# A hybrid mixer trunk on one core: the low parts of the w_up weights made by ScalarE and an accumulating DMA instead of VectorE

## The chip, the cores and the metric

One core of a Trainium2 chip runs the whole program; the other cores are idle. The metric is the device time in microseconds (us) of one execution. The engines are TensorE (PE, with its weight loads listed apart as PEld), VectorE (DVE), ScalarE (ACT), GpSimd (POOL) and SyncE (SP), which here only issues DMAs. Lower is better.

## The reference

One layer of a trunk over 512 tokens of width 1024, all in float32. Four mixers (a pooling branch, a dilated attention, a stick-breaking attention, a state-space branch) are gated and summed; then comes the feed-forward part that the change touches:

```
gu = hn @ w_up[l]                                   # 512x1024 @ 1024x5632
h = silu(gu[..., :FFN_HIDDEN]) * gu[..., FFN_HIDDEN:]
x = x + h @ w_down[l]                               # 512x2816 @ 2816x1024
return rmsnorm(x, final_norm_g)
```

## The kernel before

Every large product is done in three TensorE passes. A float32 operand is split in a high part, its value rounded to the shorter type float32r, and a low part, the float32 value minus the high part. `mm3` (L195) multiplies high by high, high by low activation, and low weight by high activation, and adds the three in one PSUM bank. For each block of 128 rows of the weight (a k tile) these are three matmuls in this order, so that the low weights are first read by the third matmul.

Weights come as a stream of chunks, listed in `specs`: those of w_in, of the gates and branches, of w_out, and then twice 11 chunks of w_up (2048 columns per partition, 1 MB) followed by 8 of w_down (1408 columns). A w_up chunk holds 8 k tiles of 256 columns; its first 128 columns make the gate product `m_fg`, the others the product `m_fu` (`s_fu` in the first two chunks). That is 24 matmuls each, 48 for a chunk; a w_down chunk is 33 matmuls into `m_d`.

`next_chunk` (L186) sets the order of the stream. When chunk c is about to be multiplied, it issues the load of a chunk two ahead into one of two `raw` buffers (`load_next`, on the queue of SP), and the split of chunk c + 1 (`split_next`) into one of two buffers `hi` and one of two `lo`. The split is done in two halves, k tiles 0 to 3 and 4 to 7: ScalarE writes `hi` with a cast, VectorE writes `lo` with a subtraction that reads `raw` and `hi`. As there are two buffers of each, the split of chunk c + 1 can't begin before TensorE is done with chunk c - 1. A `raw` buffer is loaded again when the last reader of it, so far the subtraction, is done. The order on each engine is that in which the program is written (a manual schedule).

Around a w_up chunk j the other work is `glu_up` (L1144): VectorE scales `m_fg` to `tg`, ScalarE applies Silu, VectorE scales `m_fu` to `tu` and multiplies, and the result is split in `hh` (ScalarE) and `hl` (VectorE). GpSimd does nothing but some memsets ahead of all this.

Of the kernel before, what the change touches and what calls it, by code (L numbers as in the profile page):

```python
# [13 lines left out]
AF = mybir.ActivationFunctionType  # L14
ALU = mybir.AluOpType
AX = mybir.AxisListType
PSUM = bass.MemoryType.PSUM
# [26 lines left out]
CST_CNT = 512  # L44
CST_W = CST_CNT + 64

N_SLOTS = 61  # [128, 512] tiles in the rotating pool
N_RAW = 2  # weight chunks loaded ahead
N_PM = 3  # PSUM banks of the main stream; the rest serve side work
S5_RATE = 0.9  # steps of the S5 branch per tick  # L50
SB_RATE = 1.0  # steps of the stick-breaking branch per tick
MAX_LAG = 4.0  # backlog of DVE and ACT (us) at which side work pauses
H_WAIT = 4  # ticks between the S5 rotation tables and their use
SB_T = 2  # steps from stick-breaking scores to their transposes
SB_O = 2  # steps from the transposes to the outputs
DIL_O = 1  # the same for the dilated branch
N_WARM = 8  # products on constants that bring up the PE clock while the first loads run
N_HALVED = 2  # last tiles of w_down done by token halves
BC_AT = 7  # k tiles of the last product before the first half is broadcast
W0_PIECES = {0: 1, 1: 3, 4: 2, 6: 2}  # first k tile: number of k tiles, pieces of the first weight chunk  # L60
S5_PAR = 48
S5_W = S5_PAR + 4 * 256

# [20 lines left out]
def _advance(clock, key, cost):  # L84
    clock[key] = cost + (clock[key] if key == "pe" else max(clock[key], clock["pe"]))
# [3 lines left out]
def hybrid_trunk(ctx: ExitStack, tc: tile.TileContext, a: dict, out: bass.AP):  # L89
    nc = tc.nc  # L90
    G, SY = nc.gpsimd, nc.sync
    clock = {"pe": 0.0, "v": 0.0, "a": 0.0}
    V = _Paced(nc.vector, lambda n: _advance(clock, "v", 0.09 + 1.04e-3 * n))
    A = _Paced(nc.scalar, lambda n: _advance(clock, "a", 0.20 + 0.83e-3 * n))
    PE = _Paced(nc.tensor, lambda n: _advance(clock, "pe", max(0.42e-3 * n, 0.1)))
    ctx.enter_context(tc.manual_schedule())

    gp = ctx.enter_context(tc.tile_pool(name="consts", bufs=1))
    sp = ctx.enter_context(tc.tile_pool(name="slots", bufs=N_SLOTS))
    wp = ctx.enter_context(tc.tile_pool(name="weights", bufs=2))  # L100
    sm = ctx.enter_context(tc.tile_pool(name="small", bufs=1))
    pm = ctx.enter_context(tc.tile_pool(name="pmain", bufs=N_PM, space=PSUM))
    pa = ctx.enter_context(tc.tile_pool(name="pside", bufs=8 - N_PM, space=PSUM))
    dp = ctx.enter_context(tc.tile_pool(name="scratch", bufs=1, space=DRAM))
    mixers = ExitStack()
# [5 lines left out]
    def nm_(nm):  # L111
        uid[0] += 1
        return f"{nm}_{uid[0]}"
# [11 lines left out]
    def side_ps(nm):  # L125
        return pa.tile([P, T], F32, tag="at", name=nm_("s_" + nm))
# [9 lines left out]
        V.tensor_tensor(r_(lo), src, hi, ALU.subtract)  # L136
        return r_(hi), r_(lo)

    # ------------------------------------------------------- weight stream
    specs = (  # L140
        [("w_in", 17 + c, 2048) for c in range(2)]
        + [("w_in", 2 + 3 * w + g, 2048) for g in range(3) for w in range(3)]
# [21 lines left out]
    loaded, ready = [], []  # L164
    used = [0]

    def load_next(pieces=1):
        key, i, n = specs[len(loaded)]
        raw = wp.tile([P, 2048], F32, tag="raw", name=nm_("raw"), bufs=N_RAW)
        for s in range(pieces):  # L170
            sl = slice(s * n // pieces, (s + 1) * n // pieces)
            SY.dma_start(raw[:, sl], a[key][i][:, sl])
        loaded.append((raw, n))

    def split_next(pieces=2):
        raw, n = loaded[len(ready)]
        ch = Chunk()
        ch.hi = wp.tile([P, 2048], F32R, tag="hi", name=nm_("hi"))
        ch.lo = wp.tile([P, 2048], F32R, tag="lo", name=nm_("lo"))
        ready.append(ch)  # L180
        for s in range(pieces):
            sl = slice(s * n // pieces, (s + 1) * n // pieces)
            A.copy(ch.hi[:, sl], raw[:, sl])
            V.tensor_tensor(ch.lo[:, sl], raw[:, sl], ch.hi[:, sl].bitcast(F32), ALU.subtract)

    def next_chunk():  # L186
        c = used[0]
        used[0] += 1
        while len(loaded) < min(len(ready) + N_RAW, len(specs)):
            load_next()  # L190
# [9 lines left out]
            PE.matmul(ps, wh, al, start=False, stop=False)  # L200
            PE.matmul(ps, wl, ah, start=False, stop=k == n - 1)

    # ------------------------------------------------- side work scheduling
    active = []

    def start(gen, rate=1.0):
# [3 lines left out]
    def tick(force=False):  # L210
        for e in list(active):
# [4 lines left out]
            if e[1] > 0:  # L216
                e[1] -= 1
                continue
            if max(clock["v"], clock["a"]) - clock["pe"] > MAX_LAG and not force:
                continue  # L220
# [7 lines left out]
        while e in active:  # L228
            tick(True)

    # ---------------------------------------------------------------- loads
    ones = gp.tile([P, P], F32, name="ones")
    G.memset(ones, 1.0)
    warm = gp.tile([P, 1], F32, name="warm")
# [1 line left out]
    ps = side_ps("warm")  # L236
    for _ in range(N_WARM):
        nc.tensor.matmul(ps[:, 0:P], ones, ones, start=True, stop=True)
    cols = gp.tile([P, 32], F32, name="cols")
    xr = []  # L240
    raw0 = wp.tile([P, 2048], F32, tag="raw", name=nm_("raw"), bufs=N_RAW)
    loaded.append((raw0, 2048))
    for kt in range(KT):
# [4 lines left out]
        xr.append(t)  # L248
        if kt in W0_PIECES:
            sl = slice(256 * kt, 256 * (kt + W0_PIECES[kt]))  # L250
            SY.dma_start(raw0[:, sl], a["w_in"][specs[0][1]][:, sl])
# [28 lines left out]
    def g3(kt):  # L280
        return cols[:, 16 + kt : 17 + kt]

    # ------------------------------------------------------------- rms norm
    def sumsq_add(acc, src):
        sq = slot("sq")
        A.activation(sq, src, AF.Square)
        if acc is None:
            return sq
        V.tensor_tensor(acc, acc, sq, ALU.add)
        return acc  # L290
# [35 lines left out]
            PE.matmul(ps[:, b : b + 1], acc[:, b * P : (b + 1) * P], ones[:, 0:1], start=True, stop=True)  # L326
        return ps

    # ------------------------------------------------------------- prologue
    xg = []  # L330
    ch0 = Chunk()
    ch0.hi = wp.tile([P, 2048], F32R, tag="hi", name=nm_("hi"))
# [2 lines left out]
    for kt in range(KT):  # L335
# [3 lines left out]
        xg.append((r_(hi), r_(lo)))  # L339
        if kt in W0_PIECES:  # L340
            sl = slice(256 * kt, 256 * (kt + W0_PIECES[kt]))
            A.copy(ch0.hi[:, sl], raw0[:, sl])
# [2 lines left out]
    rb8 = slot("rb8")  # L345
    env = {}

    # ------------------------------------------------- relative bias tables
    bias_d = dp.tile([12, BIAS_N], F32, name="bias_d")
    bias = {}  # L350

# [28 lines left out]
                SY.dma_start(bias[g, h], bass.AP(src.tensor, src.offset + off, [[1, P], [1, w]]))  # L380
            off += BIAS_L[g]

    # -------------------------------------------------------- S5 parameters
    s5 = cp.tile([P, S5_W], F32, name="s5p")
    are, aim, ldt = s5[:, 0:16], s5[:, 16:32], s5[:, 32:48]

# [49 lines left out]
    def s5_gen():  # L436
# [110 lines left out]
        for q in range(4):  # L547
# [52 lines left out]
            for g in range(2):  # L600
                for jr in range(4):
                    base = (g * 4 + jr) * 16
                    for tau in range(jr + 1):
# [3 lines left out]
                        )  # L607
            yield H_WAIT
            ph_re, ph_im = side_ps("hre"), side_ps("him")
# [64 lines left out]
            ys5.append(split(yg, "yg"))  # L674
            yield

    # ------------------------------------------------------ dilated attention
    def perm_out(t, g):
        if g == 0:
            return t  # L680
# [67 lines left out]
    def dil_gen():  # L748
# [51 lines left out]
        wts, yt = {}, {}  # L800
        for s in range(len(units) + 1 + DIL_O):
            if s > DIL_O and (s - DIL_O) % 2 == 0:
                hp, g, _ = units[s - 1 - DIL_O]
                po = side_ps("po")
# [38 lines left out]
                    V.tensor_scalar(st[:, o : o + kn], st[:, o : o + kn], fw[g][:, b, h : h + 1], None, ALU.mult)  # L843
            yield

    # ------------------------------------------------------- stick breaking
    sq, sk, sv = [], [], []
    m_up = cst[:, CST_UP : CST_UP + P]
    m_low = cst[:, CST_LOW : CST_LOW + P]
# [3 lines left out]
    def sb_gen():  # L853
        units = [(h, b) for h in range(4) for b in range(4)]
        bes, wts, pos = {}, {}, {}
        for s in range(len(units) + SB_T + SB_O):
            if s >= SB_T + SB_O:
                u = s - SB_T - SB_O
                h, b = units[u]
# [10 lines left out]
                if b == 3:  # L870
                    ysb.append(split(pos[h], "sb"))
            if SB_T <= s < len(units) + SB_T:
                u = s - SB_T
                h, b = units[u]
# [19 lines left out]
                V.tensor_tensor(be[:, : n - 1], be[:, : n - 1], om[:, 1:n], ALU.mult)  # L894
            yield

    # ----------------------------------------------------------------- pool
    ypool = [None] * 4
    pwt = []

# [33 lines left out]
        V.scalar_tensor_tensor(r_(lo), ps, cols[:, 24 + g : 25 + g], hi, ALU.mult, ALU.subtract)  # L934
        ypool[g] = (r_(hi), r_(lo))

    # ------------------------------------------------------------ main: w_in
    start(bias_tables())
    start(pool_load())
    e_s5 = start(s5_gen(), S5_RATE)  # L940

# [23 lines left out]
    ch = next_chunk()  # L965
# [21 lines left out]
    for g in range(3):  # L987
        for lst, scale in ((dq, rb8), (dk, rb)):
            ch = next_chunk()
# [7 lines left out]
        ch = next_chunk()  # L997
        if g < 2:
            vt = [slot("v"), slot("v")]
            for b in range(4):  # L1000
# [6 lines left out]
                    scale=rc[g][:, b : b + 1],  # L1007
# [54 lines left out]
    sb_v(1)  # L1062
    e_sb = start(sb_gen(), SB_RATE)

    # --------------------------------------------------- gates and branches
    merged = [slot("mg") for _ in range(8)]
    mg = []

# [30 lines left out]
    for c in range(2):  # L1099
        ch = next_chunk()  # L1100
# [14 lines left out]
    branch(3, yglu, last=True)  # L1115
    mixers.close()

    # ------------------------------------------------- output of the mixers
    fp = ctx.enter_context(tc.tile_pool(name="ffn", bufs=1))

    def keep(nm):
# [5 lines left out]
    for c in range(4):  # L1127
        ch = next_chunk()
# [11 lines left out]
            acc = sumsq_add(acc, t)  # L1140
    rb2 = keep("rb2")

    # ------------------------------------------------------------------ ffn
    def glu_up(psg, psu):  # L1144
        tg, tu = slot("tg"), slot("tu")
        V.tensor_tensor(tg, psg, rb2, ALU.mult)
# [6 lines left out]
    for part in range(2):  # L1153
        hid = []
        for j in range(hk * part, hk * (part + 1)):
            ch = next_chunk()
# [7 lines left out]
            if j == 0:  # L1164
                dgs = diags(inv_rms(ssq_mm(acc)[:, 0:4], 4), "r2")
                acc = None
                first = psg, psu
                continue
            hid.append(glu_up(psg, psu))
        for nt in range(8 - N_HALVED * part):  # L1170
            ch = next_chunk()
# [3 lines left out]
            if part:  # L1175
                acc = sumsq_add(acc, x2[nt])

    # ------------------------- the last tiles by token halves, final rms norm
    H = T // 2
    last = [(nt, next_chunk()) for nt in range(8 - N_HALVED, 8)]  # L1180
    pq = [side_ps("ssq"), side_ps("ssq")]
# [58 lines left out]
    nt, ch = last[-1]  # L1240
    ps = main_ps("d")
    down_half(nt, ch, 1, ps, kall[:BC_AT])
    go0()
    ssq_half(1, 0, acc, True, False)
    down_half(nt, ch, 1, ps, kall[BC_AT:])
    store_half(0, bc0, outs[:2])
# [136 lines left out]
```

## Time and profile before

| what | value |
|---|---|
| time, median of 2 runs (998.97 and 1000.77) | 999.87 us |
| profiled execution, first to last instruction | 999.0 us |
| PE busy | 986.6 us, 99% |
| DVE busy | 574.1 us, 57% |
| ACT busy | 361.5 us, 36% |
| POOL busy | 4.3 us |
| mean granted TensorE clock | 0.995 of full speed |
| DMA traffic | 100.18 MB, mean 100 GB/s |

The profiled execution's span stands 0.9 us below the median of the runs and lies between the two, so that sums made against the one hold for the other. Busy time of PE counts overlapping matmuls up to the modelled end of each; the time that a matmul takes is read from the starts of two that follow one another.

### The profile page before, as it was taken

What the parts mean: (1) busy time and instruction counts of PE and PEld (TensorE: products, weight loads), DVE (VectorE), ACT (ScalarE), POOL (GpSimd) and SP (SyncE); (2) the same over time, 40 slices, a digit from 0 to 9 for tenths busy, and PEclk for the clock granted to TensorE, in tenths of its full rate; (3) what the DMA queues carried; (4) which work ended last, traced back from release to release, by engine and by line L of the source; (5) the groups of instructions that cost most, each with busy time, mean ns of one, the idle gap of its engine ahead of it and who ended that gap; (6) DMA issues with size and microseconds to landing.
All of it is one profiled execution on the core that took longest, in us unless ns stands there. A gap on an engine that the chain in (4) does not pass through costs nothing.

```text
span 999.0 us, 12492 instructions
## 1 busy us (share of the span) xinstructions
PE 986.6 (99%) x4926; PEld 828.5 (83%) x4926; DVE 574.1 (57%) x1108; ACT 361.5 (36%) x606; POOL 4.3 (0%) x20
## 2 busy tenths in 40 slices
PE   8999999999999999999999999999999999999996
PEld 7888988988988888887888888888888888888886
DVE  6576358578877877865635565445443244454344
ACT  6253344333445444226433343332222122232231
POOL 1000000000000000000000000000000000000000
PEclk9999999999999999999999999999999999999998
DMA  7442031422112213352352323222312323222212
GB/s 270 150 139 95 9 124 52 138 73 85 64 54 69 71 49 95 119 190 92 120 176 95 117 89 125 84 85 85 114 58 99 131 85 124 87 85 87 87 59 85
DMA packets 39362, 100.18 MB, mean 100 GB/s; under 512 B 14894, under 2 KB 22747, under 8 KB 33544
## 3 DMA queue, kind: packets, MB, share of 16 engines
q1 hardware_dynamic: 39304, 99.38, 29.1%
q8 instruction: 39, 0.64, 0.2%
q14 instruction: 19, 0.16, 0.1%
HBM read 94.94 MB, written 4.42 MB: 99 GB/s over the span
## 4 chain that ended last, share of the span: by engine, by line
PE 96%; DVE 2%; ACT 1%; DMA 1%; issue 0%; SPq 0%; DVEq 0%
PE m_g L79 16%; PE m_fg L79 12%; PE m_d L79 12%; PE m_fu L79 11%; PE m_b L79 7%; PE m_qk L79 7%; PE m_v L79 5%; PE m_sqk L79 4%; PE m_o L79 4%; PE m_u L79 3%; PE m_sv L79 2%; PE s_fu L79 1%; PE m_gb L79 1%; PE m_ga L79 1%; PE s_psy L79 1%; PE s_u L79 1%
## 5 line engine op out<-in xcount | busy, mean ns | idle before, releaser
L79 DVE TENSOR_TENSOR lo<-raw,hi 128x1024 fp32r<-128x1024 f32 (+4 forms) x192 | 194.5, 1053 | 47.0 <-ACT hi L79 46.0
L79 ACT CAST hi<-raw 128x1024 fp32r<-128x1024 f32 (+4 forms) x192 | 166.1, 913 | 65.3 <-PE m_d L79 41.5
L79 PE MATMUL m_g<-xh,hi 128*128 128x512 f32 x256 | 102.6, 401 | 0.0
L79 PE MATMUL m_g<-xh,lo 128*128 128x512 f32 x256 | 100.0, 391 | 0.3 <-DVE lo L79 0.3
L79 PE MATMUL m_g<-xl,hi 128*128 128x512 f32 x256 | 99.6, 389 | 0.0
L79 PE MATMUL m_d<-hh,hi 128*128 128x512 f32 (+1 forms) x198 | 72.5, 366 | 0.0
L79 PE MATMUL m_d<-hl,hi 128*128 128x512 f32 (+1 forms) x198 | 72.4, 365 | 0.0
L79 PE MATMUL m_d<-hh,lo 128*128 128x512 f32 (+1 forms) x198 | 72.3, 365 | 0.0
L79 PE MATMUL m_fg<-x2h,hi 128*128 128x512 f32 x176 | 68.6, 390 | 0.0
L79 PE MATMUL m_fg<-x2h,lo 128*128 128x512 f32 x176 | 68.5, 389 | 0.0
L79 PE MATMUL m_fg<-x2l,hi 128*128 128x512 f32 x176 | 68.5, 389 | 0.0
L79 DVE TENSOR_TENSOR tu<-m_fu,rb 128x512 f32<-128x512 f32 x20 | 13.8, 691 | 95.0 <-PE m_fu L79 95.0
L79 PE MATMUL m_fu<-x2h,hi 128*128 128x512 f32 x160 | 62.2, 389 | 0.0
L79 PE MATMUL m_fu<-x2l,hi 128*128 128x512 f32 x160 | 62.2, 389 | 0.0
L79 PE MATMUL m_fu<-x2h,lo 128*128 128x512 f32 x160 | 62.2, 389 | 0.0
L79 ACT ACTIVATE gt<-gt 128x512 f32<-128x512 f32 x32 | 20.2, 632 | 109.1 <-DVE gt L79 109.1
L79 PEld LDWEIGHTS m_g<-xh,lo 128*128 128x128 f32 x256 | 48.0, 188 | 11.2 <-DVE lo L79 1.0
L79 PEld LDWEIGHTS m_g<-xh,hi 128*128 128x128 f32 x256 | 48.1, 188 | 10.9 <-issue 1.0
L79 PEld LDWEIGHTS m_g<-xl,hi 128*128 128x128 f32 x256 | 48.1, 188 | 10.7 <-issue 1.0
L79 ACT CAST hh<-tu 128x512 fp32r<-128x512 f32 x22 | 13.7, 622 | 113.9 <-DVE tu L79 113.9
L79 DVE TENSOR_TENSOR x<-m_d,x 128x512 f32<-128x512 f32 (+1 forms) x18 | 11.4, 632 | 65.3 <-PE m_d L79 65.3
L79 PEld LDWEIGHTS m_d<-hh,lo 128*128 128x128 f32 x198 | 37.3, 189 | 6.0
(352 smaller groups left out, 2057.6 us busy)
## 6 DMA issues: line engine op xcount, KB each, us to landing
raw<-in_w_up SPq DMA_DIRECT2D x22, 1024.0 KB, 4.7
raw<-in_w_g SPq DMA_DIRECT2D x24, 768.0 KB, 4.2
raw<-in_w_in SPq DMA_DIRECT2D x17, 1024.0 KB, 5.8
raw<-in_w_down SPq DMA_DIRECT2D x16, 704.0 KB, 4.0
raw<-in_w_g SPq DMA_DIRECT2D x8, 640.0 KB, 3.7
raw<-in_w_out SPq DMA_DIRECT2D x4, 1024.0 KB, 4.7
x<-in_x SPq DMA_DIRECT2D x8, 256.0 KB, 4.6
raw<-in_w_glu SPq DMA_DIRECT2D x2, 1024.0 KB, 7.4
```

Of the source, the lines that this page charges most:

```text
L79: return f(out, *args, **kw)
```

## The change

For chunks of w_up alone, ScalarE writes the negated weights, rounded to float32r, into `lo` (an activation Copy with scale -1), and a DMA issued from GpSimd then adds the weights to it, read once more from HBM. `lo` again holds the float32 weight minus its rounded value. The subtraction on VectorE is gone for these chunks, 44 instructions of 128x1024; 44 instructions on ScalarE and 44 DMAs of 512 KB take its place. The other chunks are split as before. Some comments are gone too.

```diff
     def split_next(pieces=2):
+        key, idx, _ = specs[len(ready)]
         raw, n = loaded[len(ready)]
         ch = Chunk()
         ch.hi = wp.tile([P, 2048], F32R, tag="hi", name=nm_("hi"))
@@
         for s in range(pieces):
             sl = slice(s * n // pieces, (s + 1) * n // pieces)
             A.copy(ch.hi[:, sl], raw[:, sl])
+            if key == "w_up":
+                A.activation(ch.lo[:, sl], raw[:, sl], AF.Copy, scale=-1.0)
+                G.dma_start(ch.lo[:, sl], a[key][idx][:, sl], accum_op=ALU.add)
+                continue
             V.tensor_tensor(ch.lo[:, sl], raw[:, sl], ch.hi[:, sl].bitcast(F32), ALU.subtract)
```

On ScalarE, while TensorE works on the third w_up chunk, this stood there before (the number behind a name is that of the buffer's use; `raw_5567` is the fourth chunk of w_up):

```order
L79 ACTIVATE tg_5641<-tg_5641 128x512 [waits DVE_49]
L79 CAST hh_5647<-tu_5642 128x512 [waits DVE_49]
L79 CAST hi_5653<-raw_5567 128x1024 [waits DMAHW5_49,PE_49,Activation_49]
L79 CAST hi_5653<-raw_5567 128x1024
L79 ACTIVATE tg_5709<-tg_5709 128x512 [waits DVE_49]
L79 CAST hh_5715<-tu_5710 128x512 [waits DVE_49]
```

And this stands there now:

```order
L79 ACTIVATE tg_5647<-tg_5647 128x512 [waits DVE_49]
L79 CAST hh_5653<-tu_5648 128x512 [waits DVE_49]
L79 CAST hi_5659<-raw_5571 128x1024 [waits DMAHW5_49,PE_49,Activation_49]
L79 ACTIVATE lo_5660<-raw_5571 128x1024 [waits DMASW3_49,DMASW2_49,PE_49]
L79 CAST hi_5659<-raw_5571 128x1024
L79 ACTIVATE lo_5660<-raw_5571 128x1024
L79 ACTIVATE tg_5717<-tg_5717 128x512 [waits DVE_49]
L79 CAST hh_5723<-tu_5718 128x512 [waits DVE_49]
```

Between the two casts and behind them stands a copy to `lo`; the Silu of the next `tg` comes two instructions later. On GpSimd's queue, where nothing stood after the memsets, these are the transfers of the second to the fifth chunk:

```order
L187 DMA lo_5490<-in_w_up 128x1024 [waits DVE_49,Activation_49]
L187 DMA lo_5490<-in_w_up 128x1024 [waits Activation_49]
L187 DMA lo_5574<-in_w_up 128x1024 [waits DMASW0_49,DMASW1_49,PE_49,Activation_49]
L187 DMA lo_5574<-in_w_up 128x1024 [waits Activation_49]
L187 DMA lo_5660<-in_w_up 128x1024 [waits DMASW3_49,DMASW2_49,Activation_49]
L187 DMA lo_5660<-in_w_up 128x1024 [waits Activation_49]
L187 DMA lo_5730<-in_w_up 128x1024 [waits DMASW5_49,DMASW4_49,Activation_49]
L187 DMA lo_5730<-in_w_up 128x1024 [waits Activation_49]
```

Each half waits for its own copy on ScalarE, so that two transfers of a chunk are issued one after the other. On TensorE, the gate product of the fourth w_up chunk began like this before:

```order
L79 MATMUL m_fg_5727<-x2h_5216,hi_5653 128x512 [waits DVE_49,Activation_49]
L79 MATMUL m_fg_5727<-x2l_5217,hi_5653 128x512
L79 MATMUL m_fg_5727<-x2h_5216,lo_5654 128x512 [waits DVE_49]
L79 MATMUL m_fg_5727<-x2h_5249,hi_5653 128x512
L79 MATMUL m_fg_5727<-x2l_5250,hi_5653 128x512
```

and now begins like this:

```order
L79 MATMUL m_fg_5737<-x2h_5216,hi_5659 128x512 [waits DVE_49,Activation_49]
L79 MATMUL m_fg_5737<-x2l_5217,hi_5659 128x512
L79 MATMUL m_fg_5737<-x2h_5216,lo_5660 128x512 [waits DMASW6_49]
L79 MATMUL m_fg_5737<-x2h_5249,hi_5659 128x512
L79 MATMUL m_fg_5737<-x2l_5250,hi_5659 128x512
```

No matmul has moved; the third of a chunk, which waited for VectorE, now waits for the first of the two transfers, and the 15th, which first reads the second half of `lo`, waits for the other in the same way.

## Rows read from the trace of the kernel before

**Rows 1.** Page, part 1: busy us, share, instructions.
```profile
PE 986.6 (99%) x4926; PEld 828.5 (83%) x4926; DVE 574.1 (57%) x1108; ACT 361.5 (36%) x606; POOL 4.3 (0%) x20
```

**Rows 2.** The chain that ended last: shares; then start, us, engine, line, tile.
```profile
PE 96%; DVE 2%; ACT 1%; DMA 1%; issue 0%; SPq 0%; DVEq 0%
...
747.19 59.84 PE m_d L79 x264
807.03 5.44 PE m_fg L79 x24
812.47 5.44 PE m_fu L79 x24
```

**Rows 3.** Waits of PE: who waited for whom, total us, times, longest.
```profile
PE s_u L79 <- ACT hi L79: 2.2, 2, 1.9
PE s_bc L79 <- DVE rr L79: 1.4, 1, 1.4
PE s_warm L238 <- POOL epsc L257: 1.0, 1, 1.0
PE s_ssq L79 <- ACT sq L79: 1.0, 1, 1.0
PE m_g L79 <- DVE lo L79: 0.3, 1, 0.3
```

**Rows 4.** Windows: stretch, length, busy of PE, PEld, DVE, ACT, POOL, clock, DMA, GB/s.
```profile
650.00:832.00 182.00, 182.00 (x804) 150.76 (x803) 75.95 (x94) 48.10 (x63) 0.00 (x0) 1.00 0.27 96
832.00:985.00 153.00, 153.00 (x730) 129.03 (x729) 67.03 (x86) 42.91 (x61) 0.00 (x0) 1.00 0.23 79
```

**Rows 5.** Timeline of PE around one w_up chunk: start, us, instruction.
```profile
823.19 0.39 PE L79 MATMUL m_fu<-x2h,hi 128*128 128x512 f32 x1
823.42 0.39 PE L79 MATMUL m_fu<-x2l,hi 128*128 128x512 f32 x1
...
828.63 0.39 PE L79 MATMUL m_fg<-x2h,hi 128*128 128x512 f32 x1
```

**Rows 6.** Timeline of ACT, w_down's last chunk and two of w_up.
```profile
799.36 2.01 ACT L79 CAST hi<-raw 128x1024 fp32r<-128x1024 f32 x2 [6.01 <-PE m_d L79]
806.84 2.01 ACT L79 CAST hi<-raw 128x1024 fp32r<-128x1024 f32 x2 [5.47 <-PE m_d L79]
...
819.47 0.62 ACT L79 CAST hh<-tu 128x512 fp32r<-128x512 f32 x1 [5.61 <-DVE tu L79]
820.00 2.00 ACT L79 CAST hi<-raw 128x1024 fp32r<-128x1024 f32 x2
824.12 0.63 ACT L79 ACTIVATE tg<-tg 128x512 f32<-128x512 f32 x1 [2.12 <-DVE tg L79]
```

**Rows 7.** Timeline of DVE in the same chunk of w_up.
```profile
821.08 2.36 DVE L79 TENSOR_TENSOR lo<-raw,hi 128x1024 fp32r<-128x1024 f32 x2 [0.26 <-ACT hi L79]
823.39 0.69 DVE L79 TENSOR_TENSOR tg<-m_fg,rb 128x512 f32<-128x512 f32 x1
```

**Rows 8.** Groups of ACT: a cast and an activation of one shape.
```profile
L79 ACT CAST hh<-tu 128x512 fp32r<-128x512 f32 x22 | 13.7, 622 | 113.9 <-DVE tu L79 113.9
L79 ACT ACTIVATE kt<-ang 128x512 f32<-128x512 f32 x4 | 2.5, 615 | 0.0
```

**Rows 9.** DMA issues: count, KB each, median us to landing.
```profile
raw<-in_w_up SPq DMA_DIRECT2D x22, 1024.0 KB, 4.7
...
raw<-in_w_g SPq DMA_DIRECT2D x8, 640.0 KB, 3.7
...
raw<-in_w_in SPq DMA_DIRECT2D x2, 512.0 KB, 6.0
...
ur<-us_d SPq DMA_DIRECT2D x4, 256.0 KB, 4.7
```

**Rows 10.** DMA in 817 to 829 us: GB/s in 40 slices of 0.3 us.
```profile
GB/s 0 0 0 0 0 0 0 0 0 0 0 0 0 0 0 0 0 0 0 0 0 55 0 0 137 137 164 164 437 437 437 437 410 437 246 55 0 0 0 0
```

**Rows 11.** Waits of SP's queue: its loads of raw.
```profile
SPq L172 <- DVE lo L79: 627.1, 74, 15.5
```

**Rows 12.** Tile raw, 600 to 999 us: issue on SP's queue, ns min/median/max.
```profile
L172 SPq DMA_DIRECT2D raw<-in_w_up x21: 327/328/328, 609.2 to 888.7; - x21
```

## The prediction

> **What bounds the kernel now.** I read the page first, then the chain of waits, the waits of each engine, the windows by stage, and the timelines of one w_up chunk. TensorE is busy for 986.6 of 999.0 us [rows 1] and holds 96% of the chain that ended last [rows 2]. The whole list of its waits is five rows, none of them in the feed-forward part [rows 3]. From 650 to 985 us it is busy without a gap at clock 1.00, the full 2.4 GHz, while VectorE works 76 of 182 us and ScalarE 48 [rows 4]. So an engine that is relieved there gives nothing back. What counts is whether the new path to `lo` is still done when TensorE wants it, and for that one needs a clock for one chunk. Matmuls start 0.227 us apart [rows 5], not the 0.39 us that one lasts. A w_up chunk is 2 x 5.44 = 10.88 us, a w_down chunk 59.84 / 8 = 7.48 [rows 2].
>
> **The clock of a chunk before.** The chunk whose `m_fu` begins at 823.19 began 5.44 us earlier, at 817.75; the next begins at 828.63 [rows 5]. Call its start 0. ScalarE reaches the split of the next chunk at 820.00, that is at 2.25, behind `hh` [rows 6]; VectorE is done with `lo` at 821.08 + 2.36 = 823.44, at 5.69 [rows 7]. TensorE reads the first half of that `lo` in the third matmul of the next chunk, at 10.88 + 2 x 0.227 = 11.33, and the second half in the 15th, at 10.88 + 14 x 0.227 = 14.05. These two are the deadlines; before, they were met with at least 5.6 and 8.3 us to spare.
>
> **VectorE's subtractions go.** 44 instructions at about 1.2 us (2.36 for a pair [rows 7]), some 52 us of an engine off the path: worth 0. A gain is excluded, since TensorE doesn't wait in this part at all [rows 3, 4].
>
> **ScalarE's copies come.** A cast and an activation of one shape cost the same, 622 and 615 ns [rows 8], and two casts of 128x1024 take 2.00 us [rows 6], so four instructions take 4.0 us in place of 2.0. The first `lo` copy is done at 2.25 + 2.0 = 4.25, the second at 6.25. Behind them waits the Silu of `tg`, which started at 824.12, at 6.37 [rows 6]: still later than 6.25. It costs 0; without that cover its own use, `tu` after the chunk's end, leaves over 4 us.
>
> **The raw load moves.** It waits for the last reader of the buffer [rows 11]; that was VectorE at 5.69 and is now ScalarE at 6.25. It lands 4.7 us later [rows 9], at 10.95, and ScalarE wants it at 10.88 + 2.25 = 13.13. Worth 0 by itself, but it now shares the DMA engines with the new transfers.
>
> **The transfers come.** The first has from 4.25 to 11.33, the second from 6.25 to 14.05. No accumulating DMA and none issued by GpSimd stands in the trace, so the price is bounded by plain ones. 640 KB land in 3.7 us and 1024 KB in 4.7 [rows 9]: 2.6 us per 1024 KB above a fixed 2.0. Of the fixed part 0.8 lies ahead of the data, as the load issued at 823.44 shows its first bytes at 824.2 [rows 7, 10]; the other 1.2 I put behind them. Lower end: the adding is free and 512 KB cost 1.3 us of the DMA engines. Upper end: 256 KB in small pieces land in 4.7 [rows 9], 2.7 above the fixed part, so 512 KB at that rate 5.4. Between: the DMA reads the weight and the old `lo`, so moves the bytes twice, 2.65; or three times, with the write not overlapped, 4.0. I take twice, as a plain copy's read and write already overlap at 437 GB/s [rows 10], and add 0.35 for the issue on GpSimd, after SP's 0.33 [rows 12]: 3.0. The one plain load of 512 KB that the page has, 6.0 us to landing [rows 9], lies among other loads and fits a price above the lower end.
>
> Two pages of the Trainium skill speak to this, and differ. DMA: Bandwidth & Descriptors, section "Anatomy of one DMA — SWDGE (gpsimd) path", prices a DMA from GpSimd at 2.0 us plus its bytes at 436 GB/s, with no word on adding; by that 512 KB would take 3.2 us, which is my lower end. Collectives: The Full Stack, section "The bandwidth ceiling", says that a reducing DMA runs at half the rate of a copying one because it reads two sources; by that it would be 2.0 + 2.4 us, near the value that I take. No run here has shown either yet.
>
> **The sum.** Loads and transfers share the engines half and half while both have data. The first transfer's data start at 4.25 + 0.8 = 5.05; by 7.05, when the raw load's start (6.25 + 0.8), it has had 2.0 of its 3.0 us; the last 1.0 takes 2.0, to 9.05; it lands at 10.25, before 11.33. The second follows at 9.05. The raw load has 1.65 left and is done at 12.35, by when the second has had 1.65; its last 1.35 end at 13.7, and it lands at 14.9. Deadline 14.05: TensorE waits 0.85 us in the 15th matmul. The raw load lands at 13.55, in time for a chunk that has become 11.73 long. How often: chunks 0, 1, 3 to 10 and 13 to 21 of w_up are prepared in a window of this form, 19 of 22; in the others ScalarE comes to the split 2 us sooner or the window is the short one of w_down. That one, where ScalarE starts at 799.36, at the window's beginning [rows 6], has its second deadline at 7.48 + 3.17 = 10.65; by the same steps the second transfer lands at 12.65, 2.0 late. In all 19 x 0.85 + 2.0 = 18.2 us, on 999.9: **1018 us**. After each wait the pattern repeats: the next split starts when TensorE frees the buffers, so a wait of one chunk isn't made good in the next.
>
> **Rivals.** (a) The adding is nearly free, 1.3 us a transfer. Then the second lands by about 11, 3 us early: nothing on the path, 1000 us. For it: the engines carry 27% in this part [rows 4], and a plain copy has room. Against: two sources must come from two memories. (b) Three passes, 4.0 us a transfer. The first then ends at 11.05 and lands at 12.25, the second ends at 15.7 and lands at 16.9, 2.85 late: 19 x 2.85 + 6 for the other windows = 60, or 1060 us, slower than before. It decides from where a transfer takes over 3.1 us of the engines, which is where the sum passes 20 us. Against it: overlap seen in plain copies; for it, nothing says that an adding engine overlaps its read and write, and every row that is slow here, the 256 KB one, goes through small pieces. (c) The transfer is cut in small pieces or added element by element, 5.4 us or more. Second transfer 5.65 late, 19 x 5.65 + 14 = 121: 1121 us, and more if GpSimd's own descriptors are the slow part, since then nothing overlaps. For it: the row of 256 KB; against: rows of 4 KB per partition are long. (d) The raw load is the one that comes late, held up behind the transfers; ScalarE then starts late and both deadlines slip. In the sum it has 0.4 us left, so this adds to (b) rather than stands alone. (e) A small gain from a calmer VectorE: TensorE has no wait to lose here [rows 3], so 998 at best.
>
> **How the numbers follow.** Chances: (a) 0.27, 1000; the forecast, prices from 2.65 to 3.4, 0.38, own range 1004 to 1036 (at 2.65 the second transfer is 0.15 late in 19 windows and 1.3 in the short one); (b) 0.20, 1040 to 1085; (c) 0.12, from 1095 on; (e) 0.03. Two per cent, 20 us, is about what a measurement of this kernel tells from no change, and the forecast's case straddles it: half of its 0.38 falls on each side. Same: 0.27 + 0.19 + 0.02 = 0.48. Slower: 0.19 + 0.20 + 0.12 = 0.51. Faster 0.01, as there is nothing to win. The range of 998 to 1100 leaves out a tenth above and next to nothing below.
>
> **What would show it.** In the profile after: subtractions of `lo` fewer by 44 and VectorE's busy time lower by about 50 us, ScalarE's higher by about 42, both without effect. PE's list of waits should have a new row, `m_fg` for the DMA `lo<-in_w_up`, with about 20 waits of 0.85 us, at the 15th matmul rather than the third; under (a) it is missing, under (b) and (c) its waits are about 3 and 6 us. The issue list should give such a transfer about 6 us to landing for the first half and 8.6 for the second; (b) has 8 and 10.7. The DMA queues should have a new one with 44 transfers, HBM reads up by 23 MB. The forecast is wrong if the wait stands at the third matmul (a latency that I didn't count), if ScalarE's copy costs clearly more than a cast, or if `raw` is late.

## The result, and the profile after

The changed kernel takes 1032.51 us (median of two runs, 1031.02 and 1034.01) against 999.87: a ratio of 1.0324 with a 95% interval of 1.028 to 1.0367. It is slower, by 32.6 us where 18 were forecast. Its profiled execution has a span of 1032.2 us.

These lines of the page of the kernel after answer to [rows 1] and the first of [rows 2], with its DMA queues between them (packets, MB, share of 16 engines):

```profile
PE 995.2 (96%) x4926; PEld 829.9 (80%) x4926; DVE 523.7 (51%) x1064; ACT 403.3 (39%) x650; POOL 42.4 (4%) x64
...
q1 hardware_dynamic: 39304, 99.38, 29.0%
q0 software_dynamic: 6336, 23.07, 12.9%
...
PE 80%; DMA 10%; ACT 3%; DVE 3%; issue 2%; POOL 1%; SPq 0%; DVEq 0%; ACTq 0%; POOLq 0%
```

VectorE has lost 50 us and ScalarE gained 42, as reckoned, both without effect. There is a new queue, and a tenth of the chain that ended last is now DMA. The waits of PE, after, against [rows 3]:

```profile
PE m_fg L79 <- DMA lo<-in_w_up: 23.8, 15, 3.3
PE s_u L79 <- ACT hi L79: 2.2, 2, 1.7
```

One row is new, and it is the one named ahead. Where in a chunk it stands is shown by a piece of the timeline of PE, with the later waits of w_up's second part behind it:

```profile
853.24 0.39 PE L79 MATMUL m_fg<-x2l,hi 128*128 128x512 f32 x1
855.55 0.50 PE L79 MATMUL m_fg<-x2h,lo 128*128 128x512 f32 x1 [1.92 <-DMA lo<-in_w_up]
855.89 0.39 PE L79 MATMUL m_fg<-x2h,hi 128*128 128x512 f32 x1
...
866.93 0.50 PE L79 MATMUL m_fg<-x2h,lo 128*128 128x512 f32 x1 [0.20 <-DMA lo<-in_w_up]
...
879.11 0.50 PE L79 MATMUL m_fg<-x2h,lo 128*128 128x512 f32 x1 [1.00 <-DMA lo<-in_w_up]
...
891.45 0.50 PE L79 MATMUL m_fg<-x2h,lo 128*128 128x512 f32 x1 [1.17 <-DMA lo<-in_w_up]
```

From 853.24 to 855.55 are 2.31 us in place of 0.227: a listed wait of 1.92 costs 2.08, since the matmul before counts as busy to its modelled end. So 0.16 is to be added to each wait. The waits have very different lengths, which the forecast didn't have. In the chain, after each long wait, ten matmuls of `m_fg` remain (start, us, engine, tile):

```profile
630.23 4.64 PE m_fg L79 x10
634.86 6.00 PE s_fu L79 x24
...
831.58 2.56 PE m_fg L79 x10
834.14 5.44 PE m_fu L79 x24
...
855.70 1.02 issue
856.73 10.16 DMA lo<-in_w_up
866.93 2.57 PE m_fg L79 x10
```

24 less 10: the wait is at the 15th matmul, the first that reads the second half of `lo`. Ten matmuls took 2.56 us there, but 4.64 after the first wait: TensorE's granted clock was lower there, 0.69 on average and then 1.00, as the windows after show (the last three columns are clock, DMA share and GB/s):

```profile
625.00:636.00 11.00, 7.74 (x23) 5.93 (x22) 1.35 (x2) 5.87 (x7) 1.72 (x2) 0.69 0.90 212
636.00:648.00 12.00, 12.00 (x63) 10.13 (x62) 1.71 (x9) 4.05 (x5) 1.72 (x2) 1.00 0.38 71
```

The transfers themselves, after: GpSimd's timeline, then time to landing by kind (the median of both halves, and the raw load of [rows 9]).

```profile
843.96 0.86 POOL L187 DMA_DIRECT2D lo<-in_w_up  x1 [13.80 <-ACT lo L79]
845.85 0.86 POOL L187 DMA_DIRECT2D lo<-in_w_up  x1 [1.03 <-ACT lo L79]
```

```profile
raw<-in_w_up SPq DMA_DIRECT2D x22, 1024.0 KB, 8.8
lo<-in_w_up POOLq DMA_DIRECT2D x44, 512.0 KB, 8.5
```

Taken one by one, the first of a pair landed 5.6 to 8.1 us after its issue, the second 8.9 to 11.2; the second one above landed 9.7 after, at 855.5, and the wait ended at 855.55. The raw load takes 8.8 us in place of 4.7. What the DMA engines did meanwhile is told by three stretches: a row of the windows (columns as in [rows 4]) and the queues of 844.5 to 855.5 us (packets, MB, share of 16 engines), then the one queue that moved data in 845.5 to 848.0 and the one in 849.5 to 851.1:

```profile
845.50:855.00 9.50, 8.13 (x36) 6.38 (x34) 2.32 (x4) 3.67 (x6) 1.03 (x2) 1.00 0.99 221
...
q0 software_dynamic: 288, 1.05, 53.7%
q1 hardware_dynamic: 144, 1.05, 31.8%
...
q0 software_dynamic: 97, 0.40, 101.5%
...
q1 hardware_dynamic: 58, 0.48, 99.9%
```

From 845.5 to 855 the engines were full (share 0.99): 5.9 us for the two transfers (53.7% of 11.0) and 3.5 for the raw load. The raw load, issued at 845.59, had moved nothing by 848.0; from 849.5 to 851.1 it had the engines to itself, although the second transfer had been issued at 845.85. For the most part the three went one behind the other.

**The account.** 23.8 us of waits and 15 x 0.16 are 26.2. TensorE's granted clock was lower behind three of them: ten matmuls took 4.64, 4.15 and 3.74 us in place of 2.56, and the 24 behind these 6.00, 5.49 and 5.90 in place of 5.44: 5.9 us in all. Together 32.1, of the 33.2 by which the spans differ; the rest isn't accounted for.

### The profile page after: what moved, and what is told of

It is laid out like the page before. It is cut to its first block, busy times and chain, and to the rows that moved or that the text cites. A ratio compares the mean times of both kernels' runs of the same rounds, so it can differ in the third digit from the quotient of the medians.

```text
span 1032.2 us, 12571 instructions
## 1 busy us (share of the span) xinstructions
PE 995.2 (96%) x4926; PEld 829.9 (80%) x4926; DVE 523.7 (51%) x1064; ACT 403.3 (39%) x650; POOL 42.4 (4%) x64
## 3 DMA queue, kind: packets, MB, share of 16 engines
q0 software_dynamic: 6336, 23.07, 12.9%
## 4 chain that ended last, share of the span: by engine, by line
PE 80%; DMA 10%; ACT 3%; DVE 3%; issue 2%; POOL 1%; SPq 0%; DVEq 0%; ACTq 0%; POOLq 0%
PE m_g L79 16%; PE m_d L79 11%; DMA lo<-in_w_up 10%; PE m_b L79 7%; PE m_qk L79 6%; PE m_fu L79 6%; PE m_fg L79 5%; PE m_v L79 4%; PE m_sqk L79 4%; PE m_u L79 3%; PE m_o L79 3%; PE m_sv L79 2%; ACT hi L79 1%; PE s_fu L79 1%; DVE tu L79 1%
## 5 line engine op out<-in xcount | busy, mean ns | idle before, releaser
L79 DVE TENSOR_TENSOR lo<-raw,hi 128x1024 fp32r<-128x1024 f32 (+5 forms) x148 | 142.7, 1004 | 42.1 <-ACT hi L79 41.4
L79 PE MATMUL m_fg<-x2h,lo 128*128 128x512 f32 x176 | 72.4, 411 | 23.8 <-DMA lo<-in_w_up 23.8
L187 POOL DMA_DIRECT2D lo<-in_w_up x44 | 38.1, 865 | 899.6 <-ACT lo L79 898.5
L79 PEld LDWEIGHTS m_fg<-x2h,lo 128*128 128x128 f32 x176 | 34.3, 195 | 37.4 <-DMA lo<-in_w_up 30.5
L79 DVE TENSOR_TENSOR tg<-m_fg,rb 128x512 f32<-128x512 f32 x22 | 15.2, 691 | 83.0 <-PE m_fg L79 78.0
```

What stands on the lines that cost most here:

```text
L79: return f(out, *args, **kw)
L187: G.dma_start(ch.lo[:, sl], a[key][idx][:, sl], accum_op=ALU.add)
```

## The experiments

Theory 1 is that of the prediction: a window, the time from one chunk's start to the next, holds two adding transfers and a raw load, which share the DMA engines, and the second transfer ends behind its deadline. Its rivals are that the latency of software-issued DMAs alone does it (2), that ScalarE's copies do (3), that the traffic does (4), and, for the sum, that each window loses a share of its own (5). The ratios are to the kernel before, timed with them: 1000.5 to 1000.8 us. Chunks of w_up are counted from 0. Edits are against the changed kernel, but those of "ScalarE's copies alone" and "The traffic alone" against the kernel before; `@@` stands for lines left out.

**ScalarE's copies alone.**

```diff
+            if key == "w_up":
+                A.activation(ch.lo[:, sl], raw[:, sl], AF.Copy, scale=-1.0)
             V.tensor_tensor(ch.lo[:, sl], raw[:, sl], ch.hi[:, sl].bitcast(F32), ALU.subtract)
```

> ScalarE's negated copies stay, but VectorE's subtraction then overwrites them and there is no transfer from GpSimd. Theory 1 (the three transfers of a window, two adding ones and the raw load, take some 9 us of the DMA engines and the second one ends too late): the copies alone cost nothing, 1000 us, no wait of TensorE in w_up. Theory 2 (the software-issued DMA's latency, GpSimd's issue included, is what is late, whatever else moves): also 1000. Theory 3 (ScalarE's extra 2 us per chunk push something late): 1010 to 1030.

1000.98 us, ratio 1.0 (0.9988 to 1.0011), no wait in w_up. The copies cost nothing; theory 3 is out. Their group in this run:

```profile
L79 ACT ACTIVATE lo<-raw 128x1024 fp32r<-128x1024 f32 x44 | 46.4, 1054 | 0.0
```

**Plain transfers.**

```diff
-                G.dma_start(ch.lo[:, sl], a[key][idx][:, sl], accum_op=ALU.add)
+                G.dma_start(ch.lo[:, sl], a[key][idx][:, sl])
```

> The same transfers from GpSimd, 44 of 512 KB with the same waits, but without the adding, so that lo receives the full weights instead of their low parts. Theory 1: a transfer takes about 1.6 us of the DMA engines in place of 3.0, the second lands near 12.4 us after a chunk's start, before its deadline of 14.05: 1000 to 1003. Theory 2: GpSimd's issue and the latency are the same, so the second transfer is as late as before: about 1030.

1010.02 us, 1.0087 (1.0069 to 1.0104), between the two. The queue's and the issues' rows of this run:

```profile
q0 software_dynamic: 6336, 23.07, 7.0%
...
raw<-in_w_up SPq DMA_DIRECT2D x22, 1024.0 KB, 8.1
lo<-in_w_up POOLq DMA_DIRECT2D x44, 512.0 KB, 5.9
```

7.0% of 16 engines over 1011.1 us, divided by 44, are 1.61 us of all engines for a transfer; with the adding it is 12.9% of 1032.2, 3.03 us. So the adding nearly doubles a transfer's time on the engines, and without it 23 of the 32.6 us are gone. (GpSimd's issue is shorter too, 0.53 us in place of 0.86, and what part of the 23 that is wasn't tried apart.) But a plain second transfer still lands 6.6 to 8.7 us after its issue, 8.1 at the median, some 2 us later than the landing expected above. The engines' share (in tenths) and the traffic of this run from 852 to 866 us, in 40 slices of 0.35 us, show where the time goes:

```profile
DMA  0000067899795896978999963321000000007469
GB/s 0 0 0 0 0 94 187 293 351 351 234 199 140 257 351 269 339 304 363 492 375 363 351 234 117 117 105 59 35 23 12 0 0 0 0 0 140 117 234 281
```

At the end, seven slices, 2.5 us, run at 117 down to 12 GB/s and at 0.3 of the engines or less: part of them is still at work while the others are idle, and the matmul that waited for the second transfer began only behind that, at 863.31. Which engines, and why, the mean doesn't show. The change's own window above has no such tail: there the engines were full to its end.

**No raw load beside them.**

```diff
@@ load_next
+        if key == "w_up":
+            if not kept:
+                kept.append(fp.tile([P, 2048], F32, tag="kept", name="kept"))
+                SY.dma_start(kept[0], a[key][i])
+            loaded.append((kept[0], n))
+            return
```

> The adding transfers as in the change, but the raw buffers of w_up aren't loaded chunk by chunk: the first w_up chunk is loaded once and stays, and ScalarE makes hi and the negated lo of every w_up chunk from it (21 loads and the true high parts are left out). Theory 1: without the 3 us of the raw load the second transfer ends near 12 and lands near 13.2, before 14.05: 1000 to 1004. Theory 2: the transfers' own latency is unchanged: about 1030.

1007.43 us, 1.006 (1.0044 to 1.0076): 80% of the loss is gone with the raw loads, which theory 2 can't explain. It isn't quite the 1000 to 1004 of theory 1. The profile has seven waits of 0.2 to 0.6 us, all in chunks of even number. The pairs of two neighbouring chunks (issue to landing, 14 first and then 15) and the engines' share for chunk 14 (836.0 to 845.2 us, slices of 0.23) say why:

```profile
lo<-in_w_up POOLq DMA_DIRECT2D x1, 512.0 KB, 6.4
lo<-in_w_up POOLq DMA_DIRECT2D x1, 512.0 KB, 7.9
...
lo<-in_w_up POOLq DMA_DIRECT2D x1, 512.0 KB, 5.5
lo<-in_w_up POOLq DMA_DIRECT2D x1, 512.0 KB, 6.2
...
DMA  0022922984998799969948995899134301220000
```

Second transfers of most even chunks land near 8.2 us after their issue, which is 6.44 + 8.2 = 14.6 on the chunk's clock, 0.6 behind the deadline. They end in a tail too, with no raw load beside them.

**Whether the source or the buffer makes the late landings.** On the kernel without raw loads, transfers that take another chunk's weights:

```diff
-                G.dma_start(ch.lo[:, sl], a[key][idx][:, sl], accum_op=ALU.add)
+                G.dma_start(ch.lo[:, sl], a[key][idx ^ 1][:, sl], accum_op=ALU.add)
```

> As the run without the raw loads, but the transfers add the neighbour chunk's weights (chunk 1's for 0, 0's for 1 and so on), so that lo is that of another chunk. Without the raw loads, transfers of even chunks landed 6.4 and 8.2 us after their issue, those of odd chunks 5.5 and 6.1. If the place in HBM makes the difference, odd chunks are now the slow ones; if the buffer that they land in does, even ones stay slow.

One run, 1011.62 us. Chunk 13 and then 14 of this run:

```profile
lo<-in_w_up POOLq DMA_DIRECT2D x1, 512.0 KB, 6.4
lo<-in_w_up POOLq DMA_DIRECT2D x1, 512.0 KB, 8.4
...
lo<-in_w_up POOLq DMA_DIRECT2D x1, 512.0 KB, 5.6
lo<-in_w_up POOLq DMA_DIRECT2D x1, 512.0 KB, 6.2
```

Now odd chunks land late, those that read the even chunks' memory. So the late landings go with the place in HBM and not with the buffer in SBUF.

**ScalarE's copies first.** Both `lo` copies ahead of both casts:

```diff
@@ split_next, ahead of the loop for the other chunks
+        if key == "w_up":
+            for s in range(pieces):
+                sl = slice(s * n // pieces, (s + 1) * n // pieces)
+                A.activation(ch.lo[:, sl], raw[:, sl], AF.Copy, scale=-1.0)
+                G.dma_start(ch.lo[:, sl], a[key][idx][:, sl], accum_op=ALU.add)
+            for s in range(pieces):
+                sl = slice(s * n // pieces, (s + 1) * n // pieces)
+                A.copy(ch.hi[:, sl], raw[:, sl])
```

> ScalarE writes both negated halves of lo ahead of the two casts to hi, so that the transfers are issued 1 and 2 us earlier; the raw buffer comes free as before. Theory 1: the engines start 1 us earlier and are through 1 us earlier, so a window that is late by 2.3 becomes late by 1.2: about 1014. Theory 2 (latency from the issue of the second transfer): 2 us earlier, so the wait all but goes: 1000 to 1005.

1015.54 us, 1.0139 (1.012 to 1.0158). On the chunk's clock the second transfer is issued 1.9 us earlier, at 4.54, but lands only 1.5 earlier at the median, and still late: from 833.0 to 841.5 us the engines' share was 0.98. More than half of the loss goes, as theory 1 has it.

**The first half alone.**

```diff
-            if key == "w_up":
+            if key == "w_up" and s == 0:
```

> Only the first half of a w_up chunk's lo is made by copy and transfer; the second half is subtracted on VectorE as before. Theory 1 (the second transfer is late because it queues behind the first and shares the engines with the raw load): the first transfer still lands 10.2 to 11.1 us after the chunk's start, before 11.33, and there is no second: 1000 to 1002. Theory 2 (any software-issued adding transfer is too slow for its deadline): half of the loss stays, about 1016.

1001.18 us, 1.0007 (0.9997 to 1.0018), and no wait in w_up. An adding DMA from GpSimd can be in time beside a raw load; the second of two in a row beside one mostly isn't.

**The traffic alone.**

```diff
+            if key == "w_up":
+                dump = fp.tile([P, 1024], F32R, tag="dump", name=nm_("dump"), bufs=3)
+                A.activation(dump, raw[:, sl], AF.Copy, scale=-1.0)
+                G.dma_start(dump, a[key][idx][:, sl], accum_op=ALU.add)
             V.tensor_tensor(ch.lo[:, sl], raw[:, sl], ch.hi[:, sl].bitcast(F32), ALU.subtract)
```

> VectorE's subtraction makes lo as before, and the same copies and 44 adding transfers go to tiles that nobody reads. Theory 1 (the loss is TensorE's wait for lo): the raw loads land later, near 9 us, ScalarE starts up to 2 us late, lo is still in time: 1000 to 1002. Theory 4 (the traffic itself slows the other engines or delays raw): 1010 or more.

1000.31 us, 0.9999 (0.9989 to 1.0008). All the transfers of the change run here, and as long as there:

```profile
raw<-in_w_up SPq DMA_DIRECT2D x22, 1024.0 KB, 9.3
dump<-in_w_up POOLq DMA_DIRECT2D x44, 512.0 KB, 8.7
```

They cost nothing while TensorE doesn't wait for them. Theory 4 is out, and with it a late raw load as the cause.

**Quarters.** `pieces = 4` for w_up:

> The split of a w_up chunk is done in four quarters instead of two halves, with 88 transfers of 256 KB. Theory 1: the engines start 1 us earlier, and the last quarter is first read by the 21st matmul, at 15.4 us instead of 14.05; it lands near 15.2: 1001 to 1006. Theory 2 (a fixed latency per transfer, in turn): four in a row take longer than two, 1030 or more.

1016.43 us, 1.0157 (1.0141 to 1.0173): outside both. The third quarter, not the fourth, is late: of chunk 13 it was issued at 832.98 and landed after

```profile
lo<-in_w_up POOLq DMA_DIRECT2D x1, 256.0 KB, 8.7
```

that is at 841.7, while the 15th matmul could have begun at 841.27. GpSimd's issue takes 0.86 us for a quarter as for a half, one behind the other at 1.04 us, which I hadn't counted: the third is issued only 2.08 us after the first. With the four copies to `lo` put first:

> Four quarters, and all four copies to lo ahead of the casts to hi. Theory 1: the first transfer is issued half a microsecond earlier than with quarters alone, the third and fourth too, and the third quarter, late by about 0.4 there, is just in time in most windows: 1004 to 1010. Theory 2 (latency per transfer, in turn): no better than quarters alone, 1016.

1008.46 us, 1.0067 (1.0049 to 1.0085), as theory 1 had it. No version beat the kernel before, and by [rows 3] none could have by much.

**Every second chunk.** First those with an odd number, then those with an even one:

```diff
-            if key == "w_up":
+            if key == "w_up" and idx % 2 == 1:
```

> Only the w_up chunks with an odd number, 11 of 22, use copy and transfer; the others are subtracted on VectorE. Theory 1 with a wait made good in the next window (a wait at the 15th matmul lengthens the time that the next chunk's transfers have): every second window had been spared by the wait of the one before, and without it each of the 11 waits its full 1.9 us, 2.8 in the short window: about 22 us and some for the clock, 1022 to 1027. Theory 5 (each window loses its own share): half of the loss, 1016.

> Only the w_up chunks with an even number use copy and transfer, the other half of the odd-numbered run. Theory 1 with a wait made good in the next window: the second transfers of even chunks land later in the change's trace (10.0 to 10.8 us after their issue), so that each wait is about 2.5 us where the window has the usual form, 8 of 11, and 3.4 in the first: some 23 us and the clock, 1024 to 1032, and this loss and that of the odd-numbered run together exceed that of the whole change by half. Theory 5 (each window loses its own share): 1008, what the odd-numbered run left of the change's loss.

1025.32 us, 1.0249 (1.0225 to 1.0272), and 1027.97, 1.0268 (1.0251 to 1.0285). Each half of the transfers costs most of what all of them cost; the two losses are 25 and 27 us, together 52 in place of 32.6. Waits of PE, odd and then even:

```profile
PE m_fg L79 <- DMA lo<-in_w_up: 18.6, 11, 2.4
```

```profile
PE m_fg L79 <- DMA lo<-in_w_up: 20.1, 9, 3.2
```

So theory 5 falls: where every chunk uses transfers, a wait of one chunk spares the next.

## Why the prediction was right, and where it wasn't

**The direction and the mechanism were right.** VectorE's relief is worth nothing, ScalarE's copies nothing, the raw load's later start nothing; the loss is TensorE's wait for the second of two transfers, at the 15th matmul, in the long and the short windows, and not at the third. In the short window of w_down 2.0 us at the 15th matmul were reckoned, and 2.78 + 0.16 measured. (By the same steps the first transfer of that window lands at 8.0, 0.07 behind the third matmul, which the sum leaves out; that weight load waited 0.44, and its matmul began 0.17 late.) The two windows that were counted as free of it, chunks 2 and 12, are. There are 15 waits where about 20 were named.

**The price of a transfer was right in part by luck.** It was put together from 2.65 us of the DMA engines, twice a plain 1.3, and 0.35 of issue. Measured are 3.03 of the engines alone, 1.9 times a plain 1.61: the factor was right, the plain price too low, and the issue stands ahead of the data. The upper end of 5.4, on which rival (c) leans, was misread: the row of 256 KB in 4.7 us is no transfer in small pieces. It moves rows of 2 KB (L664 of the kernel), and the four of that row were issued in turn with four others of 256 KB, so it shows a queue and not a price.

Of the two rules of the Trainium skill the one on two source reads (Collectives: The Full Stack, "The bandwidth ceiling") agrees with the measured ratio, 1.9. The Trainium skill's other one, 2.0 us plus the bytes for a DMA from GpSimd (DMA: Bandwidth & Descriptors, "Anatomy of one DMA — SWDGE (gpsimd) path"), gives 3.2 us, an estimate by which nothing would have been late. Measured to landing, for the first of a pair with the raw load's start beside its end: 3.8 to 5.1 us plain, 5.6 to 8.1 adding.

**The landing of the second transfer was mis-sized.** Forecast 14.9 on the chunk's clock. For the chunk prepared from 839.41 on: issued at 845.85, that is at 6.44, landed 9.7 us later, at 16.14. The trace shows which terms of the sum were off. The first data moved at about 845.5, that is at 6.1, and not at 5.05: GpSimd starts 0.3 us behind ScalarE's copy, at 843.96, and the data come some 1.6 behind that start, where 0.8 was taken in all. The engines were then full for 9.5 us, to about 855, and not for 8.65: the raw load took 3.5 of them in place of 2.65. Behind the last data stood 0.5 us and not 1.2. That is 1.1 + 0.85 - 0.7, the 1.2 us by which the landing was late. And the three didn't share the engines half and half, as in the sum, but for the most part one behind the other; with full engines the last one's end is the same. The wait of a window that starts clean is then 16.14 - 14.05 = 2.09, not 0.85; measured 1.92 + 0.16.

**The step "a wait of one chunk isn't made good in the next" was wrong.** It holds for a wait ahead of the split. This wait comes at the 15th matmul, 3.17 us into a chunk, when the next split, from 2.25 on, is already under way: it lengthens the time that the next transfers have. Each wait is what the landing gives, less the wait before. For chunks 13 to 16, with landings of 9.7, 10.2, 9.2 and 10.2 after the issue: 2.09; 2.59 - 2.08 = 0.51; 1.59 - 0.36 = 1.23; 2.59 - 1.16 = 1.43 (the landing that a clean window would give, less the measured wait before). Measured, with 0.16 added: 2.08, 0.36, 1.16, 1.33. The runs with every second chunk show the same from the other side.

**The two misses worked against each other**: waits 2.5 times as long, of which a good part were made good: 26 us in place of 18. **The clock wasn't in the sum at all**: 6 us.

Rival (a), free adding, falls by the plain transfers' run: without the adding the loss is 9 us, with it 33. Rivals (b) and (c) fall by the price of 3.03. Of (d) nothing is left: raw took 9.3 us in the run with the traffic alone, and that cost nothing. (e) falls with VectorE's 50 us, which gave nothing back.

## What to carry to other kernels

An engine that is busy but off the path has nothing to give back; what replaces its work must meet the same deadline, so write down for each stage when the buffer becomes free and when its first reader comes, and put the new path's steps between them, queue by queue. Where two transfers and a load fill the DMA engines, the last one's landing comes behind the sum of all three and not behind its own price. A wait inside a stage can give time to the work of the next that is already under way, so that waits don't simply add up.

## What the runs showed of the hardware

- An adding DMA of 512 KB takes the DMA engines 3.03 us, a plain one from GpSimd 1.61; GpSimd is busy issuing it for 0.86 us, with a plain one for 0.53.
- Transfers from GpSimd's queue and loads from SP's went for the most part one behind the other: a raw load issued at 845.59 had moved nothing by 848.0, and from 849.5 to 851.1 it alone moved data, beside a transfer issued at 845.85. In the kernel before, a raw load's data came about 1 us after its issue (823.44 to 824.2 or a little later).
- An adding DMA's first data came some 1.6 us after GpSimd began its issue (843.96 to about 845.5).
- With plain transfers the traffic of a window ended in a tail of 2.5 us in which only part of the engines moved data. The adding ones of the late stretch of HBM had one as well, with no raw load beside them; the change's window from 845.5 to 855 had none.
- With no raw load beside them, the two transfers of a chunk landed 5.5 and 6.2 us after their issue from one 1 MB stretch of HBM, 6.4 and about 8.2 from the next; the order went with the source and not with the buffer written. Why isn't settled.
- Around three waits of 2 us and more, between dense matmuls, the granted clock stood lower, at 0.69 on average over 625 to 636 us and at 0.89 over 660 to 675 and 690 to 705, so at the 1.2 GHz level for a part of each. Around others as long, at 831.58 and 855.55, it stayed at 1.00. What makes the difference wasn't tried.
